# One single-precision state product per chunk in a Mamba-2 scan, with the decayed x made on VectorE

## The chip, the core and the metric

The kernel runs on one core of a Trainium2 chip. A core has five engines, each with its own instruction stream: TensorE (PE in the profile; PEld is its weight load), VectorE (DVE), ScalarE (ACT), GpSimd (POOL) and SyncE (SP), which issues most transfers. They share the on-chip memory SBUF; TensorE writes its products to PSUM, from where DVE and ACT read them. Engines wait for one another by semaphores. The metric is the device time of one execution in microseconds (us).

## The reference

One layer of a hybrid decoder is computed for 1024 prompt tokens and 8 sequences of 8 sample tokens (1088 columns). The input projection feeds two mixers, a Mamba-2 scan and an S5 recurrence; both are projected back, gated, added, and projected out. What matters here is the chunked scan. It has 8 groups, each with 4 heads of 64 channels and a state of 128, and runs over chunks of 128 tokens:

```python
X = x.astype(jnp.float32) * dt[..., None]
A_cs = jnp.cumsum(dA, axis=-1)
Lmat = jnp.exp(jnp.where(causal, A_cs[..., :, None] - A_cs[..., None, :], -jnp.inf))
CB = jnp.einsum('bclgn,bcsgn->bgcls', Cc, Bc)
Y_diag = jnp.einsum('bgcls,bgrcls,bcsgrp->bclgrp', CB, Lmat, X)
decay_states = jnp.exp(A_cs[..., -1:] - A_cs)
states = jnp.einsum('bclgn,bgrcl,bclgrp->bcgrpn', Bc, decay_states, X)
```

The last line is the product that the change is about: each chunk adds to the state the product of B (tokens by state) with X times the decay to the chunk's end (tokens by channels). The output of a chunk needs the state that the chunk before it left.

## The kernel before

**Precision.** TensorE multiplies the type fp32r (a rounded single precision) faster than plain single precision (f32). The dense projections therefore split each operand into a rounded part and the rest (hi and lo) and add three products: hi·hi, lo·hi, hi·lo. Weights come as tiles of 128x1024; ACT makes hi (L143), DVE makes lo (L144). The state product uses the same scheme: ACT copies B into the rounded bt[0] (named b in the trace, L676), DVE makes the rest bt[1] (bt, L677), ACT copies the decayed x into xh (x, L688) and POOL makes xl (L689), and three products go into one PSUM tile (pss).

**Stages.** After the norm and the first projections come eight groups. For each, `conv_tile` runs four times (x0, x1, B, C) and `gate_tile` twice; each is a dense product of 128 output channels over all 1088 columns in blocks of 512, 288 and 288 (PSUM tiles psd), with 24 products per block. A conv tile ends in a tail. ACT copies the blocks into xp (L580, L582, L583) and starts the convolution (L589), DVE adds the three other taps (three L591), ACT takes a tanh (L592, written over xp) and DVE closes the SiLU (L593).

**The scan beside it.** `ssd` is a generator with the scan of one group, run in pieces between the blocks of the next group's projections (`drive` and `stage`; lists of counts say how many pieces follow each block). For each chunk, `prepare` is run for the next chunk, then `outputs` for this one.

- `prepare`: the cumulated decays come by DMA, broadcast over partitions, into ea (bca in the trace). TensorE transposes x0, x1 and B into one PSUM tile pt (pst) and puts B·C beside them. DVE adds the causal mask (msk, L671), ACT takes four exponentials (L673). Then bt (L676, L677), xdt = x·dt from PSUM on DVE (L679), xd = xdt·dec on POOL (L681), msk times B·C from PSUM (L682), the exponential of ea on ACT (L684) and its product with C on POOL (L685), and xh and xl from xd.
- `outputs`: four pairs of products of 64 channels make psy: msk with xdt, and ea with the state. DVE adds D·x (ysb, L743, twice). The state product follows (pss). DVE decays the state (L752) and adds pss to it (L753); in the first chunk it copies pss (L750).

A ninth chunk holds the 64 sample tokens; its B and xd are split in `stack`, which the change leaves as it was. `decays` is run once before the scan and makes dt, ncs (the negated cumulated decays) and dec (decay to the chunk's end) for all chunks and heads.

**What sets the order.** TensorE's instructions are chained in the order in which the program issues them, so a product that waits holds up all behind it. The order on ACT, DVE, POOL and SP is set by the Tile scheduler. PSUM has two tiles for pt, two for psy, one for pss and three for psd. SBUF has two buffers each for msk, bca, xdt, bt, xh and xl, and one for xd.

Of the kernel before, what the change touches and what calls it, by code (L numbers as in the profile page):

```python
# [12 lines left out]
F32 = mybir.dt.float32  # L13
F32R = mybir.dt.float32r
# [3 lines left out]
MUL, ADD, SUB, MAX, MIN = ALU.mult, ALU.add, ALU.subtract, ALU.max, ALU.min  # L18

P = 128  # L20
# [53 lines left out]
class Kernel:  # L74
# [408 lines left out]
    def decays(self, p):  # L483

        nc, pk, cn = self.nc, self.pk, self.cn
        V, S = nc.vector, nc.scalar
# [54 lines left out]
        for b in range(2):  # L541
            for j in range(4):
                self.mm(ps[32 * j:32 * j + 32, 32 * b:32 * b + 32], cn[:64, C_STRI + 32 * b:C_STRI + 32 * b + 32], da[:64, 256:],
                        start=True, stop=True)
# [16 lines left out]
        V.tensor_tensor(self.dec[:64, 256:], tots[:64, :32], self.ncs[:64, 256:], op=ADD)  # L561
        S.activation(self.dec[:, :256], self.dec[:, :256], AF.Exp)
        S.activation(self.dec[:64, 256:], self.dec[:64, 256:], AF.Exp)
        ts = self.psum("s")
        self.mm(ts[:, :256], self.ones[:64], dab.rearrange("p b h -> p (b h)"), start=True, stop=True)
        S.activation(self.etots, ts[:, :256], AF.Exp)
# [65 lines left out]
    def ssd(self, p, g, xcs, szs):  # L632

        nc, a = self.nc, self.a
        V, S, G = nc.vector, nc.scalar, nc.gpsimd
# [8 lines left out]
        h4 = lambda x: x.rearrange("p (h q) -> p h q", h=4)  # L644
# [4 lines left out]
        def prepare(c):  # L649
            smp = c == 8  # L650
            L = 64 if smp else P
            hc = c * 32 + 4 * g
            cl = slice(c * P, c * P + L)
            ea = self.t(p, [P, 4, L], "bca", 2)
            nc.sync.dma_start(ea, self.d["cs"][4 * g:4 * g + 4, cl].partition_broadcast(P))
            if smp:
                xs = []
                for src in (x0, x1, Bc, Cc):
                    d = self.t(p, [P, 64], "xsm", 4)
                    G.tensor_copy(d.rearrange("p (b t) -> p b t", t=8),  # L660
                                  src[:, 1027:].rearrange("p (b t) -> p b t", t=11)[:, :, :8])
                    xs.append(d)
            else:
                xs = [s[:, cl] for s in (x0, x1, Bc, Cc)]
            pt = self.psum("t")
            for j in range(3):
                self.tr(pt[:L, j * P:(j + 1) * P], xs[j], self.ident)
            self.mm(pt[:L, 384:384 + L], xs[2], xs[3], start=True, stop=True)
            m = self.t(p, [P, 4, L], "msk", 2)
            ng = self.cn[:64, C_SNEG:C_SNEG + 64] if smp else self.neg  # L670
            V.tensor_tensor(m[:L], ea[:L], ng.unsqueeze(1).to_broadcast([L, 4, L]), op=ADD)  # L671
            for h in range(4):
                S.activation(m[:L, h], m[:L, h], AF.Exp, bias=self.ncs[:L, hc + h:hc + h + 1])  # L673
            bt = None if smp else (self.t(p, [P, P], "b3", 2, F32R), self.t(p, [P, P], "bt", 2, F32R))
            if not smp:
                S.copy(bt[0], pt[:, 256:384])  # L676
                V.tensor_tensor(bt[1], pt[:, 256:384], bt[0].bitcast(F32), op=SUB)  # L677
            xdt = self.t(p, [P, 256], "xdt", 2)
            V.tensor_tensor(h4(xdt[:L]), h4(pt[:L, :256]), self.dt[:L, hc:hc + 4].unsqueeze(2).to_broadcast([L, 4, 64]), op=MUL)  # L679
            xd = self.t(p, [P, 256], "xd", 1)  # L680
            G.tensor_tensor(h4(xd[:L]), h4(xdt[:L]), self.dec[:L, hc:hc + 4].unsqueeze(2).to_broadcast([L, 4, 64]), op=MUL)  # L681
            V.tensor_tensor(m[:L], m[:L], pt[:L, 384:384 + L].unsqueeze(1).to_broadcast([L, 4, L]), op=MUL)  # L682
            if 0 < c < 8:
                S.activation(ea, ea, AF.Exp)  # L684
                G.tensor_tensor(ea, ea, xs[3].unsqueeze(1).to_broadcast([P, 4, L]), op=MUL)  # L685
            if not smp:
                xh, xl = self.t(p, [P, 256], "x3", 2, F32R), self.t(p, [P, 256], "xl", 2, F32R)
                S.copy(xh, xd)  # L688
                G.tensor_tensor(xl, xd, xh.bitcast(F32), op=SUB)  # L689
                xd = xh, xl  # L690
            bx = smp and [stack(h, pt[:, 256:384], xd) for h in range(2)]
            chunk[c] = (L, hc, cl, xs, ea, m, bt, xdt, xd, bx)

        def stack(h, bs, xd):


            own, other, last = (slice(32 * q, 32 * q + 32) for q in (h, 1 - h, 2))
            b3, x3 = self.t(p, [P, P], "b3", 2, F32R)[:96], self.t(p, [P, 256], "x3", 2, F32R)[:96]
            S.copy(b3[own], bs[own])
            S.copy(b3[last], bs[own])  # L700
            V.tensor_tensor(b3[other], bs[own], b3[own].bitcast(F32), op=SUB)
            S.copy(x3[own], xd[own])
            S.copy(x3[other], xd[own])
            V.tensor_tensor(x3[last], xd[own], x3[own].bitcast(F32), op=SUB)
            bx = self.t(p, [96, 4, P], "bx", 2, F32R)
            V.tensor_tensor(bx, b3.bitcast(F32).unsqueeze(1).to_broadcast([96, 4, P]),
                            self.cn[:96, C_S3:C_S3 + 4].unsqueeze(2).to_broadcast([96, 4, P]), op=MUL)
            return bx, x3
# [17 lines left out]
        def outputs(c, past=None):  # L726
            L, hc, cl, xs, ea, m, bt, xdt, xd, bx = chunk[c]
            smp = c == 8
            for q in range(2):
                yp = self.psum("y")  # L730
                two = [(2 * q + hh, yp[64 * hh:64 * hh + 64, :L]) for hh in range(2)]
                hs = lambda h: slice(64 * h, 64 * h + 64)
                for h, o in two:
                    self.mm(o, xdt[:L, hs(h)], m[:L, h], start=True, stop=c == 0)
                if smp:
                    for b in range(2):
                        for h, o in two:
                            self.mm(o[:, 32 * b:32 * b + 32], past[:, b, h],
                                    self.cn[:, :160].rearrange("p (j c) -> p j c", c=40)[:, :, :8], start=False, stop=b == 1)
                elif c > 0:  # L740
                    for h, o in two:
                        self.mm(o, state[0][:, hs(h)], ea[:, h], start=False, stop=True)
                V.scalar_tensor_tensor(ys[q][:, cl], xs[q], self.pk[:, K_DS + 2 * g + q:K_DS + 2 * g + q + 1], yp[:, :L], op0=MUL, op1=ADD)  # L743
            if not smp:
                sp = self.psum("s")
                for j, (l, m_) in enumerate(((bt[0], xd[0]), (bt[1], xd[0]), (bt[0], xd[1]))):
                    self.mm(sp[:, :256], l, m_, start=j == 0, stop=j == 2)
                new = self.t(p, [P, 256], "st", 2)
                if c == 0:
                    V.tensor_copy(new, sp[:, :256])  # L750
                else:
                    V.tensor_tensor(h4(new), h4(state[0]), self.etot[:, hc:hc + 4].unsqueeze(2).to_broadcast([P, 4, 64]), op=MUL)  # L752
                    V.tensor_tensor(new, new, sp[:, :256], op=ADD)  # L753
                state[0] = new
                if c == 7:
                    nc.sync.dma_start(a["ssm_p"][g], new)
                return

        def round_(r):
            bx, x3 = chunk[8][-1][r]  # L760
            for tag, b in ((("s", 0), ("t", 2)), (("y", 0), ("y", 2)))[r]:
# [4 lines left out]
                V.tensor_tensor(sv, sv, sp, op=ADD)  # L766

        prepare(8)
        yield
        past = earlier()  # L770
        yield
        if self.sums:
            self.sums()
            yield
        outputs(8, past)
        yield
        for r in range(2):
            round_(r)
            yield
        nc.sync.dma_start(a["ssm_s"][g], s0)  # L780
        self.s0 = load(g + 1) if g < 7 else None
        prepare(0)
        yield
        for c in range(8):
            if c < 7:
                prepare(c + 1)
                yield
            outputs(c)
            yield
# [771 lines left out]
```

## Time and profile before

| | |
|---|---|
| median of 3 runs | 1764.91 us (1763.91 to 1765.38) |
| the profiled execution | 1763.57 us |
| its span | 1761.4 us |
| granted TensorE clock, mean | 0.994 |
| ACT | 39% busy |
| DVE | 67% busy |
| POOL | 24% busy |

The page gives the busy time of each engine and a chain that ended last. Rows of a timeline give the start and the length of an instruction in us, the engine, the line, the operation, and what it writes and reads; in square brackets stands the idle time before it and who ended it. L61 is the helper through which all products go, so products are told apart by their tiles. Successive products overlap, so the time from start to start is what one costs.

### The profile page before, as it was taken

Reading aid. Unit: us, or ns where it says so; the run is one execution under the profiler, and the core shown is the slowest. Engines: PE = TensorE matmul, PEld = TensorE weight load, DVE = VectorE, ACT = ScalarE, POOL = GpSimd, SP = SyncE. Lnnn points to the kernel's source line nnn. Section 1 sums busy time; section 2 is a strip of 40 time slices with the busy share of each in tenths; the row PEclk is TensorE's granted clock in tenths of the full one; section 3 lists DMA queues with packets and bytes.
Section 4 is the critical chain, followed back from the end, with each engine's and each line's share of the span. In section 5 each row is a group of like instructions: output and inputs, shape, how many; then the busy total and the mean of one; then the engine's idle time right before and its main releaser. Section 6 shows DMA issues by size and latency. Waiting matters only on the chain.

```text
span 1761.4 us, 31495 instructions
## 1 busy us (share of the span) xinstructions
PE 1719.2 (98%) x12510; PEld 1559.5 (89%) x12510; DVE 1176.7 (67%) x1976; ACT 685.4 (39%) x1414; POOL 425.1 (24%) x588
## 2 busy tenths in 40 slices
PE   9999999999999999999999999999999999999996
PEld 8997888889888888888878888888899989999996
DVE  6899977636586777778676877754565723485444
ACT  6422222223354544545444445445632302242221
POOL 0013212100143333424243333332341000022014
PEclk9999999999999999999999999999999999999998
DMA  5334343442132223232332222334523855474522
GB/s 209 96 103 117 103 152 106 126 143 76 54 105 91 91 79 121 62 126 61 87 107 80 100 89 96 108 117 147 165 98 122 259 175 195 132 226 137 197 97 75
DMA packets 138690, 212.62 MB, mean 121 GB/s; under 512 B 14832, under 2 KB 95120, under 8 KB 136496
## 3 DMA queue, kind: packets, MB, share of 16 engines
q1 hardware_dynamic: 138544, 210.62, 37.3%
q8 instruction: 98, 1.61, 0.4%
q14 instruction: 48, 0.39, 0.1%
HBM read 158.55 MB, written 52.03 MB: 120 GB/s over the span
## 4 chain that ended last, share of the span: by engine, by line
PE 70%; DVE 14%; DMA 5%; ACT 5%; issue 3%; POOL 2%; SPq 0%; POOLq 0%; ACTq 0%; DVEq 0%
PE psd L61 59%; PE psy L61 5%; PE pst L61 4%; DVE xc L591 4%; DMA bca<-d_cs 2%; PE pss L61 2%; POOL xd L681 2%; DMA yz<-d_yz 1%; ACT xp L592 1%; DVE xc L593 1%; DVE wlo L144 1%; DVE msk L671 1%; ACT msk L673 1%; DVE hl L61 1%; DVE cm L61 1%
## 5 line engine op out<-in xcount | busy, mean ns | idle before, releaser
L61 PE MATMUL psd<-hh,whi 128*128 128x512 f32 (+2 forms) x1872 | 619.9, 331 | 1.7 <-ACT zt L627 1.5
L61 PE MATMUL psd<-hh,wlo 128*128 128x512 f32 (+2 forms) x1872 | 608.0, 325 | 0.0
L61 PE MATMUL psd<-hl,whi 128*128 128x512 f32 (+2 forms) x1872 | 608.0, 325 | 0.0
L61 PEld LDWEIGHTS psd<-hh,whi 128*128 128x128 f32 x1872 | 352.7, 188 | 37.1 <-issue 9.4
L61 PEld LDWEIGHTS psd<-hl,whi 128*128 128x128 f32 x1872 | 352.3, 188 | 23.9
L61 PEld LDWEIGHTS psd<-hh,wlo 128*128 128x128 f32 x1872 | 352.8, 188 | 21.5
L144 DVE TENSOR_TENSOR wlo<-raw,whi 128x1024 fp32r<-128x1024 f32 (+1 forms) x139 | 171.7, 1236 | 149.8 <-ACT whi L143 149.6
L143 ACT CAST whi<-raw 128x1024 fp32r<-128x1024 f32 (+1 forms) x139 | 144.8, 1043 | 166.4 <-PE psd L61 106.4
L591 DVE SCALAR_TENSOR_TENSOR xc<-xp,pk,xc 128x1112 f32<-128x1112 f32 x96 | 149.6, 1558 | 20.3 <-ACT xc L589 19.0
L61 PE MATMUL psd<-ynh,whi 128*128 128x272 f32 x512 | 148.6, 290 | 0.0
L61 PE MATMUL psd<-ynl,whi 128*128 128x272 f32 x512 | 147.7, 288 | 0.0
L61 PE MATMUL psd<-ynh,wlo 128*128 128x272 f32 x512 | 147.3, 288 | 0.0
L673 ACT ACTIVATE msk<-msk,ncs 128x128 f32<-128x128 f32 (+1 forms) x288 | 93.3, 387 | 125.4 <-DVE msk L671 122.0
L685 POOL TENSOR_TENSOR bca<-bca,xc 128x512 f32<-128x512 f32 x56 | 85.0, 1518 | 130.4 <-ACT bca L684 121.4
L1325 POOL TENSOR_TENSOR fs<-fs,zt 128x272 f32<-128x272 f32 x24 | 26.2, 1090 | 336.6 <-ACT zt L1323 239.9
L61 PEld LDWEIGHTS psd<-ynh,whi 128*128 128x128 f32 x512 | 96.4, 188 | 0.3
L61 PEld LDWEIGHTS psd<-ynh,wlo 128*128 128x128 f32 x512 | 96.3, 188 | 0.1
L61 PEld LDWEIGHTS psd<-ynl,whi 128*128 128x128 f32 x512 | 96.2, 188 | 0.0
L681 POOL TENSOR_TENSOR xd<-xdt,dec 128x256 f32<-128x256 f32 (+1 forms) x72 | 58.4, 812 | 143.5 <-DVE xdt L679 105.3
L671 DVE TENSOR_TENSOR msk<-bca,cn 128x512 f32<-128x512 f32 (+1 forms) x72 | 53.6, 745 | 43.7 <-DMA bca<-d_cs 43.3
L61 PE MATMUL psd<-mh,wlo 128*128 128x272 f32 x256 | 73.8, 288 | 0.0
L61 PE MATMUL psd<-ml,whi 128*128 128x272 f32 x256 | 73.8, 288 | 0.0
(372 smaller groups left out, 3224.2 us busy)
## 6 DMA issues: line engine op xcount, KB each, us to landing
raw<-wt SPq DMA_DIRECT2D x143, 512.0 KB, 3.9
bca<-d_cs SPq DMA_DIRECT2D x64, 256.0 KB, 3.5
d_yz<-ysb SPq DMA_DIRECT2D x16, 544.0 KB, 3.4
yz<-d_yz SPq DMA_DIRECT2D x32, 272.0 KB, 4.5
s<-s SPq DMA_DIRECT2D x8, 1024.0 KB, 4.8
ssm_s<-s SPq DMA_DIRECT2D x8, 1024.0 KB
x<-xt SPq DMA_DIRECT2D x16, 272.0 KB, 5.6
d_ud<-ub SPq DMA_DIRECT2D x8, 544.0 KB, 3.6
```

Source lines behind the costliest of these rows:

```text
L61: ins = f(*args, **kw).ins
L143: S.copy(hi, raw)
L144: V.tensor_tensor(lo, raw, hi.bitcast(F32), op=SUB)
L591: V.scalar_tensor_tensor(xc[:, :W], xp[:, j:j + W], cw(j), xc[:, :W], op0=MUL, op1=ADD)
L592: S.activation(xp[:, :W], xc[:, :W], AF.Tanh)
L593: V.scalar_tensor_tensor(xc[:, :W], xp[:, :W], 1.0, xc[:, :W], op0=ADD, op1=MUL)
L671: V.tensor_tensor(m[:L], ea[:L], ng.unsqueeze(1).to_broadcast([L, 4, L]), op=ADD)
L673: S.activation(m[:L, h], m[:L, h], AF.Exp, bias=self.ncs[:L, hc + h:hc + h + 1])
L681: G.tensor_tensor(h4(xd[:L]), h4(xdt[:L]), self.dec[:L, hc:hc + 4].unsqueeze(2).to_broadcast([L, 4, 64]), op=MUL)
L685: G.tensor_tensor(ea, ea, xs[3].unsqueeze(1).to_broadcast([P, 4, L]), op=MUL)
L1325: G.tensor_tensor(total[q], total[q], sq[:, :nb], op=ADD)
```

## The change

Three things change. `decays` multiplies dec by dt once, for all chunks (two DVE products, one for the prompt's columns and one for the sample's). In `prepare`, xd is made by DVE straight from the transposed x in PSUM and the new dec, with two buffers, and no longer by POOL from xdt. And the state product takes B and xd in single precision: one ACT copy of B (f32), no split of B or xd, and one product into pss. The sample chunk's xd is made by DVE too.

```diff
         S.activation(self.dec[:64, 256:], self.dec[:64, 256:], AF.Exp)
+        V.tensor_tensor(self.dec[:, :256], self.dec[:, :256], self.dt[:, :256], op=MUL)
+        V.tensor_tensor(self.dec[:64, 256:], self.dec[:64, 256:], self.dt[:64, 256:], op=MUL)
...
-            bt = None if smp else (self.t(p, [P, P], "b3", 2, F32R), self.t(p, [P, P], "bt", 2, F32R))
+            bt = None if smp else self.t(p, [P, P], "bt", 2)
             if not smp:
-                S.copy(bt[0], pt[:, 256:384])
-                V.tensor_tensor(bt[1], pt[:, 256:384], bt[0].bitcast(F32), op=SUB)
+                S.copy(bt, pt[:, 256:384])
...
-            xd = self.t(p, [P, 256], "xd", 1)
-            G.tensor_tensor(h4(xd[:L]), h4(xdt[:L]), self.dec[:L, hc:hc + 4].unsqueeze(2).to_broadcast([L, 4, 64]), op=MUL)
+            xd = self.t(p, [P, 256], "xd", 2)
+            V.tensor_tensor(h4(xd[:L]), h4(pt[:L, :256]), self.dec[:L, hc:hc + 4].unsqueeze(2).to_broadcast([L, 4, 64]), op=MUL)
...
-            if not smp:
-                xh, xl = self.t(p, [P, 256], "x3", 2, F32R), self.t(p, [P, 256], "xl", 2, F32R)
-                S.copy(xh, xd)
-                G.tensor_tensor(xl, xd, xh.bitcast(F32), op=SUB)
-                xd = xh, xl
...
-                for j, (l, m_) in enumerate(((bt[0], xd[0]), (bt[1], xd[0]), (bt[0], xd[1]))):
-                    self.mm(sp[:, :256], l, m_, start=j == 0, stop=j == 2)
+                self.mm(sp[:, :256], bt, xd, start=True, stop=True)
```

The order of the instructions moves with it. Lines of the changed kernel are numbered anew: the taps L591 are L593 there, the tanh L592 is L594, the block copy L580 is L582, the closing product L593 is L595.

On ScalarE, at the tail of a group's third conv tile (B; it is the place W2 of the prediction, whose psd, psy, pss, pst and xc these rows name with numbers), there stands before, from the start of the convolution (L589) to the tanh (L592; b and x are the rounded parts of B and xd, whi a weight's):

```order
L589 ACTIVATE xc_7969<-xp_7818,pk_70 128x1112
L673 ACTIVATE msk_7983<-msk_7983,ncs_4709 128x128
L676 CAST b_1357_7989<-pst_7978 128x128
L684 ACTIVATE bca_7976<-bca_7976 128x512
L143 CAST whi_8216<-raw_8215 128x1024
L688 CAST x_1361_8000<-xd_7995 128x256
L580 COPY xp_8004<-psd_8013 128x512
L592 ACTIVATE xp_7818<-xc_7969 128x1112
```

and in the changed kernel at the same place:

```order
L591 ACTIVATE xc_7821<-xp_7680,pk_70 128x1112
L675 ACTIVATE msk_7835<-msk_7835,ncs_4709 128x128
L678 COPY bt_7841<-pst_7830 128x128
L685 ACTIVATE bca_7828<-bca_7828 128x512
L143 CAST whi_8044<-raw_8043 128x1024
L582 COPY xp_7850<-psd_7859 128x512
L594 ACTIVATE xp_7680<-xc_7821 128x1112
```

The copy of xd is gone; the block copy now follows the weight's cast, and the tanh follows the block copy as before.

On VectorE, at the same place, from behind the first of the three taps to the state's update, before:

```order
L677 TENSOR_TENSOR bt_7990<-pst_7978,b_1357_7989 128x128
L591 SCALAR_TENSOR_TENSOR xc_7969<-xp_7818,pk_70,xc_7969 128x1112
L679 TENSOR_TENSOR xdt_7993<-pst_7978,dt_4708 128x256
L591 SCALAR_TENSOR_TENSOR xc_7969<-xp_7818,pk_70,xc_7969 128x1112
L682 TENSOR_TENSOR msk_7983<-msk_7983,pst_7978 128x512
L743 SCALAR_TENSOR_TENSOR ysb_7499<-xc_6572,pk_70,psy_8039 128x128
L743 SCALAR_TENSOR_TENSOR ysb_7500<-xc_6730,pk_70,psy_8045 128x128
L593 SCALAR_TENSOR_TENSOR xc_7969<-xp_7818,xc_7969 128x1112
L753 TENSOR_TENSOR st_8055<-st_8055,pss_8051 128x256
```

and in the changed kernel:

```order
L680 TENSOR_TENSOR xdt_7843<-pst_7830,dt_4708 128x256
L593 SCALAR_TENSOR_TENSOR xc_7821<-xp_7680,pk_70,xc_7821 128x1112
L682 TENSOR_TENSOR xd_7845<-pst_7830,dec_4710 128x256
L593 SCALAR_TENSOR_TENSOR xc_7821<-xp_7680,pk_70,xc_7821 128x1112
L683 TENSOR_TENSOR msk_7835<-msk_7835,pst_7830 128x512
L739 SCALAR_TENSOR_TENSOR ysb_7373<-xc_6510,pk_70,psy_7885 128x128
L739 SCALAR_TENSOR_TENSOR ysb_7374<-xc_6662,pk_70,psy_7891 128x128
L595 SCALAR_TENSOR_TENSOR xc_7821<-xp_7680,xc_7821 128x1112
L748 TENSOR_TENSOR st_7899<-st_7899,pss_7897 128x256
```

Where bt and xdt stood between the taps, xdt and xd stand now; the rest keeps its order.

On TensorE, at the same place, a chunk's outputs and the first product of the projection's next block (psd_8058), before:

```order
L61 MATMUL psy_8039<-msk_7900,xdt_7910 64x128 x2
L61 MATMUL psy_8039<-bca_7893,st_7937 64x128 x2
L61 MATMUL psy_8045<-msk_7900,xdt_7910 64x128 x2
L61 MATMUL psy_8045<-bca_7893,st_7937 64x128 x2
L61 MATMUL pss_8051<-x_1346_7917,b_1342_7906 128x256
L61 MATMUL pss_8051<-x_1346_7917,bt_7907 128x256
L61 MATMUL pss_8051<-xl_7918,b_1342_7906 128x256
L61 MATMUL psd_8058<-hh_3_148,whi_8008 128x288
```

and in the changed kernel, where that block is psd_7902:

```order
L61 MATMUL psy_7885<-msk_7760,xdt_7768 64x128 x2
L61 MATMUL psy_7885<-bca_7753,st_7789 64x128 x2
L61 MATMUL psy_7891<-msk_7760,xdt_7768 64x128 x2
L61 MATMUL psy_7891<-bca_7753,st_7789 64x128 x2
L61 MATMUL pss_7897<-xd_7770,bt_7766 128x256
L61 MATMUL psd_7902<-hh_3_148,whi_7854 128x288
```

Three rows of pss became one; nothing else moved on this engine.

## The prediction

> **What bounds the kernel now.** I read the page first (engine shares, chain), then a stretch of the scan by window, then TensorE's waits in the scan, then the timeline around each kind of wait.
>
> The page's busy line, its chain by engine, and the window from 660 to 755 us, which is one group of heads (columns: length; busy and instruction count of PE, PEld, DVE, ACT, POOL; clock; DMA share; GB/s):
>
> ```profile
> PE 1719.2 (98%) x12510; PEld 1559.5 (89%) x12510; DVE 1176.7 (67%) x1976; ACT 685.4 (39%) x1414; POOL 425.1 (24%) x588
> PE 70%; DVE 14%; DMA 5%; ACT 5%; issue 3%; POOL 2%; SPq 0%; POOLq 0%; ACTq 0%; DVEq 0%
> 660.00:755.00 95.00, 92.80 (x677) 81.69 (x676) 72.04 (x109) 46.34 (x106) 35.05 (x46) 1.00 0.28 92
> ```
>
> TensorE is the bound, with 92.8 of 95 us busy, so DVE (76%), ACT (49%) and POOL (37%) matter only where TensorE waits for them. Its waits in the scan (470 to 1235 us; total, times, longest):
>
> ```profile
> PE psy L61 <- DVE st L753: 8.5, 8, 2.2
> PE psy L61 <- DVE st L750: 3.7, 6, 1.4
> PE psy L61 <- DVE ysb L743: 2.6, 6, 1.2
> PE psy L61 <- DVE msk L682: 1.9, 1, 1.9
> ```
>
> Together 16.7 us. All are the product of a chunk's output (psy) waiting for the scan's DVE work; the change can win these, and no more, plus what it does to TensorE's own work.
>
> **TensorE's own work.** Three rounded products become one of single precision. Single precision with 256 columns on 128 partitions occurs once before the scan, each product as two records; the first two rows are the same product seen with one and with both records, then another, and then the three products that go:
>
> ```profile
> 453.89 0.38 PE L61 MATMUL pst<-ysb,cn 128*128 128x256 f32 x1
> 453.89 0.59 PE L61 MATMUL pst<-ysb,cn 128*128 128x256 f32 x2
> ...
> 454.64 0.48 PE L61 MATMUL psy<-ysb,cn 128*128 128x256 f32 x1
> 454.64 0.70 PE L61 MATMUL psy<-ysb,cn 128*128 128x256 f32 x2
> ...
> 719.02 0.39 PE L61 MATMUL pss<-x,b 128*128 128x256 f32 x1
> 719.24 0.28 PE L61 MATMUL pss<-x,bt 128*128 128x256 f32 x1
> 719.36 0.28 PE L61 MATMUL pss<-xl,b 128*128 128x256 f32 x1
> 719.48 0.49 PE L61 MATMUL pst<-cn,xc 128*128 128x128 f32 x3
> ```
>
> A record's tail overlaps the next, so cadence counts. In the first product the second record adds 0.59 - 0.38 = 0.21 us. In the second product, whose first record shows its weight load (0.48 against 0.38, so 0.10), the second starts 0.70 - 0.38 = 0.32 after the first. The old three run from 719.02 to 719.48, 0.46 us, and their first shows the load too (0.39 against 0.28). So the new product takes 0.32 + 0.22 = 0.54: +0.08 us, over 8 groups x 8 chunks **+5.1 us**. Bounds: both loads hidden, 0.43, -0.03 x 64 = -1.9; both exposed, 0.64, +0.18 x 64 = +11.5. I take the middle, since the place (behind 64-column products with other weights) is that of the old first product.
>
> **What goes and comes on the other engines.** Five groups by shape (busy and mean ns; then idle ahead), and the DVE row behind the decays:
>
> ```profile
> L677 DVE TENSOR_TENSOR bt<-pst,b 128x128 fp32r<-128x128 f32 x64 | 18.1, 283 | 7.3 <-ACT b L676 6.8
> L679 DVE TENSOR_TENSOR xdt<-pst,dt 128x256 f32<-128x256 f32 x64 | 26.4, 413 | 0.0
> L688 ACT CAST x<-xd 128x256 fp32r<-128x256 f32 x64 | 25.8, 403 | 103.0 <-POOL xd L681 102.9
> L689 POOL TENSOR_TENSOR xl<-xd,x 128x256 fp32r<-128x256 f32 x64 | 53.8, 841 | 25.8 <-ACT x L688 25.8
> L679 DVE TENSOR_TENSOR xdt<-pst,dt 64x256 f32<-64x256 f32 x8 | 3.3, 417 | 27.7 <-PE pst L61 27.7
> ...
> 462.58 0.69 DVE L607 SCALAR_TENSOR_TENSOR sz<-zt,psd 128x512 f32<-128x512 f32 x1 [5.14 <-ACT zt L606]
> ```
>
> DVE loses bt (0.283) and gains xd, which has the form of xdt (0.413): +0.13 us a chunk, +8.3 in all. No row has that product with dec; below, it could cost as little as bt (0), above, as much as an operation slowed by a busy POOL (the 1.78 against 1.32 further down: 0.56, so +0.28). I take 0.13, the same operation on the same operands' sizes. ACT loses 25.8, POOL xl's 53.8 and xd. Busy time alone wins nothing, as TensorE is the bound. The two added products in the decays cost at most 2 x 0.41; DVE is idle for 5.14 us behind them, so nothing; without that cover +0.8. The ACT copy in place of the cast lies early in a chunk and is as large. The sample chunk's xd moves from POOL to DVE, 8 x 0.42; DVE idles 27.7 us for TensorE ahead of these eight, so I take nothing (if it all counted, +3.3).
>
> **Where the waits come from.** A group's second to fourth conv tiles each have a tail: three L591 on DVE, tanh L592 on ACT, L593 on DVE. Behind L593 on DVE stands the state (L750 or L753), and for that TensorE waits. Third tile of a group, the W2 place:
>
> ```profile
> 711.36 0.44 PE L61 MATMUL psy<-msk,xdt 128*64 128x128 f32 x4
> ...
> 712.60 1.36 DVE L591 SCALAR_TENSOR_TENSOR xc<-xp,pk,xc 128x1112 f32<-128x1112 f32 x1
> 712.82 1.62 POOL L681 TENSOR_TENSOR xd<-xdt,dec 128x256 f32<-128x256 f32 x1 [1.65 <-DVE xdt L679]
> 714.47 0.41 ACT L688 CAST x<-xd 128x256 fp32r<-128x256 f32 x1 [3.95 <-POOL xd L681]
> 714.78 0.58 ACT L580 COPY xp<-psd 128x512 f32<-128x512 f32 x1
> 715.25 1.14 ACT L592 ACTIVATE xp<-xc 128x1112 f32<-128x1112 f32 x1
> 716.42 1.32 DVE L593 SCALAR_TENSOR_TENSOR xc<-xp,xc 128x1112 f32<-128x1112 f32 x1 [1.35 <-ACT xp L592]
> 717.66 0.41 DVE L753 TENSOR_TENSOR st<-st,pss 128x256 f32<-128x256 f32 x1
> 718.22 0.44 PE L61 MATMUL psy<-bca,st 128*64 128x128 f32 x4 [1.13 <-DVE st L753]
> ```
>
> The last L591 ends at 713.96; with 0.12 of handover L592 could start at 714.08. It starts at 715.25, **1.17 late**, since ACT stands for 3.95 us at L688 (waiting for POOL's xd, 1.62 us) and L580 stands behind. L580's source was complete when psy started at 711.36. In the new order L688 is gone and L580 runs in that idle time. So L593, the state and psy come 1.17 earlier, less 0.13 for xd ahead of the last L591: 1.04. TensorE arrives 0.08 later: the wait loses 1.12, all but its last hundredth. Six groups have it so and the first group once (listed under L743): 7 x 1.12 = **-7.8** out of 8.5 + 1.2 us.
>
> Second tile, W1:
>
> ```profile
> 695.73 1.37 DVE L591 SCALAR_TENSOR_TENSOR xc<-xp,pk,xc 128x1112 f32<-128x1112 f32 x1
> ...
> 697.60 0.41 ACT L688 CAST x<-xd 128x256 fp32r<-128x256 f32 x1 [2.13 <-POOL xd L681]
> 697.91 1.13 ACT L592 ACTIVATE xp<-xc 128x1112 f32<-128x1112 f32 x1
> ...
> 700.78 0.44 PE L61 MATMUL psy<-bca,st 128*64 128x128 f32 x4 [0.71 <-DVE st L750]
> ```
>
> Only L688 stands ahead: L592 could start at 697.22 and is 0.69 late; less 0.13, plus 0.08, it gives 0.64, or what the wait holds. Six waits make 3.7; I take **-3.5**.
>
> Fourth tile, W3, where the new POOL has no xl:
>
> ```profile
> 736.91 1.78 DVE L593 SCALAR_TENSOR_TENSOR xc<-xp,xc 128x1112 f32<-128x1112 f32 x1 [0.15 <-ACT xp L592]
> 738.03 1.25 POOL L689 TENSOR_TENSOR xl<-xd,x 128x256 fp32r<-128x256 f32 x1 [0.52 <-ACT x L688]
> 739.69 0.44 PE L61 MATMUL psy<-msk,xdt 128*64 128x128 f32 x4 [0.21 <-DVE ysb L743]
> ```
>
> L593 takes 1.78 beside xl and 1.32 without (716.42): 0.46 in five groups, **-2.3**, part of it in the state wait that follows. The row that should carry it is L743 (2.6, of which 1.2 belong to W2).
>
> **The clock.** The longest of these waits, the window behind it (0.50 is the granted clock), and the first wait of the scan:
>
> ```profile
> 910.65 0.44 PE L61 MATMUL psy<-bca,st 128*64 128x128 f32 x4 [2.19 <-DVE st L753]
> ...
> 910.97:914.38 3.41, 3.41 (x22) 3.08 (x18) 3.33 (x9) 2.52 (x8) 1.08 (x2) 0.50 0.23 42
> ...
> 499.03 0.66 PE L61 MATMUL psy<-msk,xdt 128*64 128x128 f32 x8 [1.93 <-DVE msk L682]
> ```
>
> A gap of 2.19 is followed by 3.41 us at half clock, a loss of 1.7; the gap of 1.93 is not. At 910.65 the wait shrinks to about 1.07, so **-1.7**. At 499.03 xd stands ahead of msk and the gap grows by 0.13 to 2.06, between a gap that kept the clock and one that did not: **+0.1**. [...]
>
> **Sum:** 5.1 - 7.8 - 3.5 - 2.3 - 1.7 + 0.1 = -10.1. The profiled execution took 1763.57 (span 1761.4), so 1753.5; the median of the runs, 1764.91, lies 1.34 above it, so **1754.8**.
>
> **Rivals.**
> 1. *The tail is late all the same* (slower). If L592 waits for something other than L688 (L580 for its block, or DVE itself), no wait shrinks and each of the 20 grows by xd's 0.13: 5.1 + 2.6 + 1.34 on 1763.57, so 1772.6. This decides where L580's block ends after POOL's xd did, at 714.44; the rows have it ended at 711.4, which speaks against it. Chance 0.09.
> 2. *Half the waits go*, since other work late in a tile (a transfer of bca, a weight cast ahead of L580) takes L688's place: -6.8 in place of -13.6, with the half clock gone or not, 1761.6 to 1763.3, and some us to both sides with the share that goes. For it: 2.19 against 1.13 at the same place shows that something else makes waits longer. Chance 0.15.
> 3. *The product costs its bounds:* hidden 1747.8, 0.03; exposed 1761.2, 0.05.
> 4. *A half clock stays or returns* at 499: 1756.5, chance 0.10.
> 5. *One product has the price of one record and its load*, 0.32: -0.14 x 64 = -9.0 in place of +5.1, so 1740.7. Both records of 0.21 stand in the trace; chance 0.02. [...]
>
> That the change doesn't do as it says is excluded by the order of instructions: one product, no xl, no L688.
>
> **Numbers.** My forecast has 0.56. Faster by over 0.2% (about what a measurement of this kernel can tell from no change) is below 1761.4: forecast, rival 4, rival 5, most of 3 and a third of 2, 0.79; slower is rival 1, 0.09; the rest 0.12. The range, 1748 to 1766, takes in the product's bounds, xd's on 13 waits (-1.7 to +2.0) and rival 2.
>
> **What would show it.** State products 0.54 apart, start to next start; ACT's L592 0.12 behind the last L591 in tiles two and three; the waits for the state at L750 and L753 below 4 us together (12.2 now); L593 at 1.32 in the fourth tile; no half clock near 910. I'd be wrong if L580 or the cast were found waiting where L688 was, or if the product took 0.6.

## The result, and the profile after

| | before | changed |
|---|---|---|
| median of 5 runs each | 1764.91 us (1760.68 to 1768.62) | 1752.61 us (1747.15 to 1754.31) |
| ratio, 95% interval | | 0.9925 [0.9902, 0.9948] |
| the profiled execution | 1763.57 us | 1750.75 us |
| its span | 1761.4 us | 1749.0 us |

The changed kernel is 12.3 us faster; 10.1 were forecast. The page of the changed kernel, its busy line and its chain by engine, and the window from 660 to 755 us (columns as before):

```profile
PE 1718.9 (98%) x12446; PEld 1558.4 (89%) x12446; DVE 1184.1 (68%) x1986; ACT 665.1 (38%) x1350; POOL 311.0 (18%) x452
PE 83%; DVE 8%; DMA 3%; ACT 2%; issue 2%; POOL 0%; SPq 0%; POOLq 0%; ACTq 0%; DVEq 0%
660.00:755.00 95.00, 95.00 (x679) 83.73 (x678) 73.22 (x111) 44.24 (x99) 22.39 (x30) 1.00 0.29 94
```

TensorE's busy time is nearly the same, its share of the chain went from 70% to 83%, and in this window it has no idle time left (2.2 us before). TensorE's waits in the changed kernel, from 470 to 1235 us (total, times, longest):

```profile
PE psy L61 <- DVE msk L683: 2.1, 1, 2.1
PE psd L61 <- ACT zt L629: 1.3, 1, 1.3
PE psy L61 <- DVE st L748: 0.9, 2, 0.7
PE psy L61 <- DVE ysb L739: 0.2, 1, 0.2
```

The waits for the state fell from 12.2 us to 0.9. The timeline of the place that the prediction called W2 (third conv tile of the same group; L593 taps, L582 block copy, L594 tanh, L595 closing product, L748 state; this timeline and those below show only the rows that the argument needs):

```profile
708.59 0.59 ACT L582 COPY xp<-psd 128x512 f32<-128x512 f32 x1 [1.08 <-PE psd L61]
709.67 1.36 DVE L593 SCALAR_TENSOR_TENSOR xc<-xp,pk,xc 128x1112 f32<-128x1112 f32 x1
711.15 1.14 ACT L594 ACTIVATE xp<-xc 128x1112 f32<-128x1112 f32 x1 [1.97 <-DVE xc L593]
712.31 1.32 DVE L595 SCALAR_TENSOR_TENSOR xc<-xp,xc 128x1112 f32<-128x1112 f32 x1 [0.17 <-ACT xp L594]
713.55 0.41 DVE L748 TENSOR_TENSOR st<-st,pss 128x256 f32<-128x256 f32 x1
713.85 0.44 PE L61 MATMUL psy<-msk,xdt 128*64 128x128 f32 x4
714.12 0.43 PE L61 MATMUL psy<-bca,st 128*64 128x128 f32 x4
```

The block copy is done before the last tap begins, the tanh starts 0.12 us behind that tap's end (711.03), and psy takes the state with no idle time. In 31 of the 32 conv tiles of this trace the tanh starts 0.11 or 0.12 us behind the last tap, in one 0.40. The new product, in the timeline of the changed kernel:

```profile
616.29 0.70 PE L61 MATMUL pss<-xd,bt 128*128 128x256 f32 x2
616.63 0.48 PE L61 MATMUL psd<-hh,whi 128*128 128x288 f32 x1
616.96 0.30 PE L61 MATMUL psd<-hh,wlo 128*128 128x288 f32 x1
617.09 0.29 PE L61 MATMUL psd<-hl,whi 128*128 128x288 f32 x1
```

Here one must not read the price off the next row's start. The first psd is recorded 0.34 us behind pss, but then lasts 0.48, and its successor starts 0.33 behind it, where 0.13 is usual (617.09 - 616.96). From 616.29 to 616.96, less 0.13, gives **0.54 us**. Against the same products in the trace before, the time from the state product's start to the sixth product behind it grew by 0.078 us in the median of the 64 chunks.

The longest of the old waits and the window around it, then the first wait of the scan and the window behind that:

```profile
901.40 0.44 PE L61 MATMUL psy<-bca,st 128*64 128x128 f32 x4 [0.71 <-DVE st L748]
...
900.00:905.00 5.00, 4.29 (x39) 3.68 (x39) 4.92 (x10) 2.40 (x8) 1.68 (x4) 1.00 0.08 16
...
498.88 1.12 PE L61 MATMUL psy<-msk,xdt 128*64 128x128 f32 x8 [2.12 <-DVE msk L683]
...
498.65:502.07 3.42, 3.19 (x13) 2.51 (x14) 3.34 (x9) 1.62 (x4) 0.00 (x0) 0.50 0.52 149
```

The half clock behind the first is gone (1.00 in the window); one of 3.41 us behind the second has come (0.50).

### The profile page after: what moved, and what is told of

It is laid out like the page before. It is cut to its first block, busy times and chain, and to the rows that moved or that the text cites. A ratio compares the mean times of both kernels' runs of the same rounds, so it can differ in the third digit from the quotient of the medians.

```text
span 1749.0 us, 31101 instructions
## 1 busy us (share of the span) xinstructions
PE 1718.9 (98%) x12446; PEld 1558.4 (89%) x12446; DVE 1184.1 (68%) x1986; ACT 665.1 (38%) x1350; POOL 311.0 (18%) x452
## 4 chain that ended last, share of the span: by engine, by line
PE 83%; DVE 8%; DMA 3%; ACT 2%; issue 2%; POOL 0%; SPq 0%; POOLq 0%; ACTq 0%; DVEq 0%
PE psd L61 69%; PE psy L61 6%; PE pst L61 5%; PE pss L61 3%; DVE xc L593 1%; DMA bca<-d_cs 1%; DMA yz<-d_yz 1%; DVE cm L61 1%; DVE hl L61 1%; ACT yg L1160 1%; DVE wlo L144 1%; DVE x L61 1%; ACT msk L675 0%; DVE xc L595 0%; DMA x<-xt 0%
## 5 line engine op out<-in xcount | busy, mean ns | idle before, releaser
L61 PE MATMUL psd<-hh,whi 128*128 128x512 f32 (+2 forms) x1872 | 630.2, 337 | 1.6 <-ACT zt L629 1.3
L144 DVE TENSOR_TENSOR wlo<-raw,whi 128x1024 fp32r<-128x1024 f32 (+1 forms) x139 | 170.4, 1226 | 145.0 <-ACT whi L143 144.9
L593 DVE SCALAR_TENSOR_TENSOR xc<-xp,pk,xc 128x1112 f32<-128x1112 f32 x96 | 149.2, 1554 | 20.9 <-ACT xc L591 17.9
L61 PE MATMUL psd<-mh,whi 128*128 128x272 f32 x256 | 73.8, 288 | 0.0
L673 DVE TENSOR_TENSOR msk<-bca,cn 128x512 f32<-128x512 f32 (+1 forms) x72 | 47.3, 658 | 38.8 <-DMA bca<-d_cs 38.6
```

Of the source, the lines that this page charges most:

```text
L61: ins = f(*args, **kw).ins
L144: V.tensor_tensor(lo, raw, hi.bitcast(F32), op=SUB)
L593: V.scalar_tensor_tensor(xc[:, :W], xp[:, j:j + W], cw(j), xc[:, :W], op0=MUL, op1=ADD)
```

## The experiments

Twelve runs were made, of ten new kernels and two that had run already, in three groups; within a group on the same chip, beside the kernel before (medians 1763.72, 1763.76 and 1764.80 us).

### What holds the tanh back: ACT's copy, or a busy POOL?

The kernel before, with the copy xh moved to POOL:

```diff
-                S.copy(xh, xd)
+                G.tensor_copy(xh, xd)
```

> The kernel before, with one edit: the rounded copy xh of the decayed x is made by POOL in place of ACT; the order on DVE, the three rounded products, POOL's xd and xl all stay. Theory A (ACT's queue: the copy that waits for POOL's xd stands ahead of the block copy and the tanh): the tanh starts 0.12 us behind the last tap in every tile, TensorE's waits for the state (L750 and L753 together 12.2 us before) fall below 3 us, and the time falls by 8.2 + 3.5 + 1.7 (half clock near 910) less 0 to 3 for a POOL that is busy beside L593 for longer: 1751 to 1755. Theory B (POOL's load: DVE is slowed by a busy POOL, and the change gained by taking 112 us of work from POOL): POOL has more work here, so no gain, 1765 or more, and the waits for the state stay at 12 or grow. Theory C (DVE making xd from PSUM is what brings the state earlier): no change, 1765.

Measured: 1750.7 us, ratio 0.9916 [0.9893, 0.9938]. The tanh starts 0.12 us behind the last tap in 31 of 32 tiles. The wait for the state at L753 in this kernel:

```profile
PE psy L61 <- DVE st L753: 2.4, 5, 1.1
```

and L750 is not among its waits any more. So the whole gain comes with one copy off ACT, with three rounded products, no xd on DVE, and more work on POOL (473.9 us busy, 425.1 before). Theory B isn't all wrong: beside the longer POOL work, L593 took 1.64 us in most second and third tiles, where 1.32 was usual (in the trace before, 1.62 to 1.78 in the seven tiles where POOL's xd and xl ran beside it, 1.31 or 1.32 in the other 25). Still the time fell, so that costs less than the lateness did.

The changed kernel, with POOL's product made again and read by nobody:

```diff
+            if not smp:
+                x2 = self.t(p, [P, 256], "x2", 1)
+                G.tensor_tensor(h4(x2), h4(xdt), self.dec[:, hc:hc + 4].unsqueeze(2).to_broadcast([P, 4, 64]), op=MUL)
```

> The changed kernel, and POOL again makes the product xdt x dec in each chunk (128x256), which nobody reads. Theory A: the load on POOL alone costs nothing that TensorE sees: waits for the state below 2 us, time as the changed kernel's, 1752.6 within 3. Theory B: POOL has 58 to 100 us of its 114 us back, so at least half of the gain of 12 is lost: 1758 or more.

Measured: 1752.01 us, ratio 0.9923 [0.9901, 0.9945], waits for the state 1.0 us. This puts back about half of the work that the change took from POOL (363.0 us busy, 311.0 in the changed kernel, 425.1 before); the copy on POOL had left all of it and added some. POOL's load is not where the time came from.

### A miss: the stall put back, and nothing happened

To that, ACT's copy:

```diff
+            if not smp:
+                x4 = self.t(p, [P, 256], "x3", 2, F32R)
+                S.copy(x4, x2)
```

> The kernel of the run with POOL's unread product, and ACT copies that product in each chunk, at the place where it copied xd before; nobody reads the copy. Only the queue on ACT differs from that run. Theory A: the tanh is 1.2 us late in third tiles and 0.7 in second tiles again, the waits for the state come back to 10 to 14 us, and the time rises by 7 x 1.17 + 6 x 0.65 = 12 us, with the half clock near 910 14: 1764 to 1768. Theory B: as the run with POOL's unread product. Theory C (the product's price is all): as the changed kernel, 1752.6.

Measured: 1751.5 us, ratio 0.9927 [0.9902, 0.9951], waits for the state 1.1 us. My theory had given 1764 to 1768. The timeline of the third tile shows why (L685 POOL's product, L692 ACT's copy):

```profile
709.50 1.68 POOL L685 TENSOR_TENSOR x<-xdt,dec 128x256 f32<-128x256 f32 x1
710.97 1.39 DVE L593 SCALAR_TENSOR_TENSOR xc<-xp,pk,xc 128x1112 f32<-128x1112 f32 x1
711.22 0.41 ACT L692 CAST x<-x 128x256 fp32r<-128x256 f32 x1 [2.33 <-POOL x L685]
711.53 0.58 ACT L582 COPY xp<-psd 128x512 f32<-128x512 f32 x1
712.45 1.13 ACT L594 ACTIVATE xp<-xc 128x1112 f32<-128x1112 f32 x1 [0.34 <-DVE xc L593]
```

ACT stands at the copy as before, and the block copy behind it, but the block copy ends at 712.11, 0.34 us ahead of the tanh. POOL's product ends at 711.18, while the last tap still runs to 712.36. In the kernel before, POOL's xd ended at 714.44 and the last tap at 713.96. What had moved is xdt, from which POOL works: with bt gone from DVE, xdt stands behind the first tap and no longer behind the second.

So the tanh was late because a **chain**, xdt behind the second tap, POOL's xd, ACT's copy, block copy, ended after the last tap. Two kernels test that. First the same kernel with POOL's product made from xd, which stands behind the second tap:

```diff
-                G.tensor_tensor(h4(x2), h4(xdt), self.dec[:, hc:hc + 4].unsqueeze(2).to_broadcast([P, 4, 64]), op=MUL)
+                G.tensor_tensor(h4(x2), h4(xd), self.dec[:, hc:hc + 4].unsqueeze(2).to_broadcast([P, 4, 64]), op=MUL)
```

> As the run with ACT's copy behind POOL's unread product, but that product is made from xd, which DVE issues behind the second tap, in place of xdt, which it issues behind the first. Theory A, refined: POOL's product ends after the last tap again, the tanh is late by 0.6 to 1.3 us in second and third tiles, the waits for the state are 9 to 14 us, and the time is 1763 to 1768. If a chain over POOL and ACT does not matter at all (as the first run with it could be read): 1752, waits below 3.

Measured: 1762.67 us, ratio 0.9993 [0.9982, 1.0003]. The third tile, and then the waits:

```profile
711.83 1.36 DVE L593 SCALAR_TENSOR_TENSOR xc<-xp,pk,xc 128x1112 f32<-128x1112 f32 x1
712.05 1.61 POOL L685 TENSOR_TENSOR x<-xd,dec 128x256 f32<-128x256 f32 x1 [1.65 <-DVE xd L682]
713.69 0.41 ACT L692 CAST x<-x 128x256 fp32r<-128x256 f32 x1 [3.95 <-POOL x L685]
714.49 1.13 ACT L594 ACTIVATE xp<-xc 128x1112 f32<-128x1112 f32 x1
```

```profile
PE psy L61 <- DVE st L754: 6.3, 6, 1.9
PE psy L61 <- DVE st L751: 2.7, 5, 1.4
```

The last tap ends at 713.19, and the tanh starts 1.30 us behind it in place of 0.12, 1.18 late as before the change; ACT idles the same 3.95 us, 9.0 us of waits are back, and the time is that of the kernel before within the interval. Between the two kernels only the input of one POOL instruction differs.

Second, the reverse: the kernel **before**, with nothing but bt and xdt exchanged on DVE.

```diff
                 S.copy(bt[0], pt[:, 256:384])
-                V.tensor_tensor(bt[1], pt[:, 256:384], bt[0].bitcast(F32), op=SUB)
             xdt = self.t(p, [P, 256], "xdt", 2)
...
+            if not smp:
+                V.tensor_tensor(bt[1], pt[:, 256:384], bt[0].bitcast(F32), op=SUB)
```

> The kernel before, with two DVE instructions of each chunk exchanged: xdt is issued ahead of the rest of B (bt), so that in the tails xdt stands behind the first tap and bt behind the second; nothing else moves. The run with ACT's copy behind POOL's unread product kept its tanh in time, and there xdt stood behind the first tap. Theory A, refined (the tanh is late because the chain from xdt behind the second tap over POOL's xd to ACT's copy ends after the last tap): POOL's xd starts 1.4 to 1.7 us earlier, ACT's copy is over before the last tap, the waits for the state fall below 3 us, TensorE's work stays: 1763.7 - 12 - 0 to 1.7 = 1750 to 1752. If the copy's place in ACT's queue alone made the tanh late, whenever its input came, or if xd must be on DVE: 1764, waits of 12.

Measured: 1748.0 us, ratio 0.9906 [0.9890, 0.9922]. The third tile (L678 xdt, L682 xd on POOL, L689 ACT's copy), and the waits:

```profile
704.79 0.41 DVE L678 TENSOR_TENSOR xdt<-pst,dt 128x256 f32<-128x256 f32 x1
705.99 1.68 POOL L682 TENSOR_TENSOR xd<-xdt,dec 128x256 f32<-128x256 f32 x1
707.33 1.52 DVE L591 SCALAR_TENSOR_TENSOR xc<-xp,pk,xc 128x1112 f32<-128x1112 f32 x1
707.71 0.41 ACT L689 CAST x<-xd 128x256 fp32r<-128x256 f32 x1 [2.33 <-POOL xd L682]
708.95 1.14 ACT L592 ACTIVATE xp<-xc 128x1112 f32<-128x1112 f32 x1 [0.34 <-DVE xc L591]
```

```profile
PE psy L61 <- DVE st L754: 1.1, 2, 0.8
PE psy L61 <- DVE st L751: 0.6, 1, 0.6
```

The copy is over before the tap ends at 708.85, and the waits for the state fall from 12.2 to 1.7 us. Two instructions exchanged give all that the change gave, with the same instructions on POOL and ACT as before.

### The two halves of the change, and TensorE's price

The kernel before with xd made by DVE from PSUM with dec x dt, split and rounded products kept:

> The kernel before with one part of the change: xd is made by DVE from PSUM with dec x dt; the split of xd and B (ACT, POOL, DVE) and the three rounded products stay. Theory A: ACT's copy waits for DVE and not for POOL, so the waits for the state go below 3 us as in the changed kernel; TensorE keeps the product at 0.46 us in place of 0.54, -5.0; POOL's xl stays beside L593, +2.3: 1752.6 - 5.0 + 2.3 = 1750, between 1747 and 1753. If the single-precision product cost nothing or less against the three (its lower bound), 1755 or more. If the single product was what removed the waits (the state comes one product earlier), 1765 and waits of 12.

Measured: 1749.8 us, ratio 0.9915 [0.9892, 0.9937], waits for the state 2.4 us.

The kernel before with the single-precision product and no split, xd kept on POOL (the expression for xd unchanged, two buffers):

> The kernel before with the other half of the change: one single-precision product of B and xd, no split of either, while xd is still made by POOL from xdt. Theory A: ACT no longer waits for POOL, so the waits for the state go as in the changed kernel; TensorE pays 5.0 for its product; DVE has 0.41 less in each chunk: 1749 to 1753. If it takes DVE's xd from PSUM to win, 1764 + 5 = 1769.

Measured: 1749.15 us, ratio 0.9912 [0.9898, 0.9926], waits for the state 0.2 us. Each half alone removes most or all of the waits (12.2 us before): the first since ACT's copy then follows a DVE instruction and stands behind the tanh in the second to fourth tiles of the last seven groups, the second since the copy is gone.

The price of the product: the changed kernel with B and xd rounded as they are written, so that one rounded product remains. It leaves the rests of B and xd out of the state.

```diff
-            bt = None if smp else self.t(p, [P, P], "bt", 2)
+            bt = None if smp else self.t(p, [P, P], "b3", 2, F32R)
...
-            xd = self.t(p, [P, 256], "xd", 2)
+            xd = self.t(p, [P, 256], "xd", 1) if smp else self.t(p, [P, 256], "x3", 2, F32R)
```

> The changed kernel with B and xd rounded to fp32r by the instructions that write them, so that one rounded product takes the place of the single-precision one; the rests of B and xd are left out of the product, and the order of all engines is that of the changed kernel. If the single-precision product takes 0.54 us and a rounded one with its load 0.22: -0.32 x 64 = -20.5, less 0 to 4 us of new waits since TensorE comes 0.32 earlier to each state: 1732 to 1737. If it takes the price of one record and its load, 0.32: -6.4, 1746. If TensorE were not the bound in the scan: 1752.

Measured: 1728.64 us, ratio 0.9807 [0.9788, 0.9825]. The product in its timeline:

```profile
602.61 0.39 PE L61 MATMUL pss<-x,b 128*128 128x256 f32 x1
602.84 0.29 PE L61 MATMUL psd<-hh,whi 128*128 128x288 f32 x1
```

0.23 us, with no long record behind it: 0.31 less than single precision, 20 us over 64. From ratio to ratio against the changed kernel (0.9925, and 0.9916 when run again) it is 19 to 21 us. Expected were 1732 to 1737, so somewhat less; almost no new waits came (1.7 us for the state). The scan is TensorE's to the last tenths, and 0.54 us is the price.

### Order in the first chunk, and one more order on VectorE

The changed kernel with the line that makes xd moved behind the one that finishes msk (L683):

> The changed kernel with xd issued behind msk (L683) in place of ahead of it. Where the first chunk's output waits for msk (2.12 us near 499 in the changed kernel, followed by 3.41 us at half clock), the wait should fall by xd's 0.33 to 0.41, to about 1.75, which kept the full clock before the change (1.93 did): -0.4 - 1.7 = -2.1 there, 1750.5 in all, if the tails elsewhere don't move; that is less than the time can tell, so the row of this wait and the clock behind it decide. If the half clock near 499 has nothing to do with the length of this gap, it stays.

Measured: 1748.98 us, ratio 0.9917 [0.9902, 0.9932], no half clock near 499 (products of 512 columns start 0.23 us apart from 498.19 to 498.88, as at full clock). But the first chunk's wait is gone altogether, 2.12 us and not 0.4: the scheduler also put a weight's rest (L144, 1.2 us on DVE) behind this chunk. The test therefore doesn't tell what xd ahead of msk costs.

The kernel before with xdt, msk, bt in this order on DVE:

```diff
-                V.tensor_tensor(bt[1], pt[:, 256:384], bt[0].bitcast(F32), op=SUB)
...
             V.tensor_tensor(m[:L], m[:L], pt[:L, 384:384 + L].unsqueeze(1).to_broadcast([L, 4, L]), op=MUL)
+            if not smp:
+                V.tensor_tensor(bt[1], pt[:, 256:384], bt[0].bitcast(F32), op=SUB)
```

> The kernel before with xdt, then msk, then the rest of B (bt) on DVE: the exchange of the two DVE instructions and the order that took the first chunk's wait away in the run with xd behind msk, together. The wait near 499 (1.66 us in the run with the exchange alone) goes, and with the state ahead of L593 the last waits for the state (1.7) too: 3 us below that run, 1744 to 1747, and the fastest of all that compute the reference. If the order behind the second tap matters only in the first chunk, 1.7 below: 1746.

Measured: **1744.93 us, ratio 0.9887 [0.9874, 0.9901]**, the lowest median of those that leave nothing out. The wait near 499 stayed at 1.8 us, against what I expected (here the weight's rest stayed ahead). The waits for the state are 0.3 us, since in second and third tiles the state now stands ahead of L593. On the same chip ran the changed kernel and the exchange alone:

> The changed kernel itself, to stand beside the next runs on the same chip. 1750 to 1754; ratio to before 0.9925 as at first.

Measured: 1750.21 us, ratio 0.9916 [0.9903, 0.9930].

> The kernel before with xdt and bt exchanged, once more, beside the changed kernel. Theory A: both are free of the waits for the state, and the changed kernel pays 64 x 0.078 = 5.0 us for its product and has lost POOL's xl beside L593 (5 x 0.26): so this one is 3 to 5 us faster, 1746 to 1749. If the first result was luck of that chip, both are equal.

Measured: 1748.26 us, ratio 0.9904 [0.9889, 0.9919]. The exchange alone and the changed kernel can't be told apart by these intervals, though by the ratios the exchange is ahead both times, by 3 and by 2 us, where 3 to 5 were expected. The version with msk ahead of bt is ahead of the changed kernel: their intervals don't overlap. Those of it and of the exchange alone do overlap, so its lead of 3 us there is not shown.

## Why the prediction was right, point by point

- **TensorE bounds the scan, so only its waits and its own work count.** Right: 20 us taken from TensorE's products came off the time, and POOL's work, half put back in one run and added to in another, did not show.
- **The product, +5.1 us.** Right: 0.078 x 64 = 5.0, from two products that stood before the scan and the middle between two bounds. The rival that priced one record and its load is out.
- **The tails, W2 and W1, -7.8 and -3.5.** The place, the lateness (1.18 us in third tiles and 0.70 in second ones where the late chain was put back) and the cure were right. Incomplete was the reason, that L580 and the tanh stand behind a copy that waits for POOL. That held only because xdt stood behind the second tap: with xdt one tap earlier the same queue did no harm. Since the change moves xdt too, it would have removed the waits even with the copy kept.
- **The size of the waits' end was too small.** From the end of the scan's first wait to the last state product, 499.03 to 1213.80 before and 498.88 to 1199.88 after, the scan lost 13.8 us. With +5.0 for the product and one half-clock stretch in each, the waits gave 18.8; the forecast had 13.6 for W1, W2 and W3. I had priced W1 and W2 by the tanh's lateness. Nearly every wait went whole: in this stretch the listed idle time of psy for DVE fell from 14.8 to 1.1 us. Each wait that goes also returns the overlap of a product with the one ahead, by my estimate some 0.17 us (713.85 + 0.44 - 714.12), 2.9 us for the 17 waits that went (20 before, 3 after). That makes 16.6; smaller waits inside this stretch that I had not counted (for POOL's xl and bca, and one of psy for ACT's zt) give 1.2. Some 1 us I can't assign. Four of the runs, too, came out below the times expected of them, by 0.3 to 3.4 us.
- **The sum was helped by luck.** The waits gave 5.2 us more than forecast, the clock 1.6 less, and behind the scan the changed execution lost 1.5 us again, in a part that takes 546.4 to 550.8 us over the traces of all runs. These misses cancel in part, so the sum (-12.4 between the spans, -10.1 forecast) came out closer than the waits by themselves did.
- **W3, -2.3.** L595 takes 1.32 us in the fourth tiles, in place of 1.78: right. The five waits for ysb there, 1.4 us together, shrank to one of 0.17; with four overlaps of 0.17 that is about 1.9. No run takes this term by itself.
- **The clock, -1.7 and +0.1.** The half clock at 910 went. The fourth rival, a half clock at 499, came true in the profiled execution (0.50 from 498.65 to 502.07), and so the clock gave nothing. I had gone by the gap's length; alone it didn't tell, since of two gaps of 2.06 us one was followed by half clock and one by full clock (last section).
- **Slower by L580 or DVE** did not occur: the copy's idle time had been there to use, and xd's 415 ns on DVE (413 forecast) did not show in the waits.

## What to carry to other kernels

When an engine waits late in a stage, follow the chain back to where its first input is issued: there an exchange of two short instructions on VectorE was worth as much as the whole change. Price the end of a wait by the whole wait, overlap included, and not only by the delay that one has found. Part of the cost of the product in single precision stood in the record behind it (0.48 us long, with its successor 0.33 behind it where 0.13 is usual), so measure to the second product that follows.

## What the runs showed of the hardware

In these runs the length of a gap alone did not tell whether half clock followed. The first wait of the scan, at the same place in the program, was 2.12 us in the changed kernel and 1.7 when run again, and across the runs a gap of 2.06 was followed by half clock in one kernel and by full clock in another. These rows are the wait and the window behind it (0.50 or 1.00 is the clock), first with the copy on POOL, then with POOL's unread product:

```profile
500.49 0.66 PE L61 MATMUL psy<-msk,xdt 128*64 128x128 f32 x8 [2.06 <-DVE msk L682]
501.73:505.14 3.41, 3.37 (x9) 2.69 (x9) 3.00 (x5) 1.63 (x5) 3.19 (x5) 0.50 0.69 216
```

```profile
500.62 0.66 PE L61 MATMUL psy<-msk,xdt 128*64 128x128 f32 x8 [2.06 <-DVE msk L686]
500.80:504.20 3.40, 3.40 (x21) 2.74 (x19) 3.40 (x8) 1.67 (x6) 0.89 (x3) 1.00 0.49 147
```

In the second run of the exchange a gap of 2.42 us kept the full clock, longer than the 2.19 that was followed by half clock before the change:

```profile
499.15 0.66 PE L61 MATMUL psy<-msk,xdt 128*64 128x128 f32 x8 [2.42 <-DVE msk L683]
499.20:502.60 3.40, 3.32 (x20) 2.58 (x21) 3.30 (x8) 1.86 (x5) 2.47 (x4) 1.00 0.55 149
```

In the traces before and after the change there are three half-clock stretches each between 130 and 1700 us, and each lasts 3.41 us. What else decided whether one followed, these rows don't show.
